# A DiT block's query projection: four full products per band pair against seven products of halves, with the projections before attention in another order

## The chip, the cores and the metric

The kernel runs on one core of a Trainium2 chip. The metric is the device time of one execution in microseconds (us). A core has a TensorE (PE; its weight loads are listed as PEld), a VectorE (DVE), a ScalarE (ACT), a GpSimd (POOL) and a SyncE (SP). All five have in-order instruction queues. SP's queue does nothing but start DMAs here; ACT and POOL start some too.

## The reference

One layer of a diffusion transformer on 1024 latent tokens and 256 context tokens, width 1024, all in float32:

```
h_x = rmsnorm(x)*(1+sc1)+sh1;   h_c = the same of ctx          # sh, sc, gt: a vector times w_mod
u, q, k, v = split(h_x @ w_in)  (512 columns each); k_c, v_c = the same of h_c
attn = neighbourhood_attention(q, k, v, k_c, v_c, rpb)          # 8 heads of 64, clamped 8 x 16 window + context keys
mix  = concat(pool_mixer(u), attn) @ w_out                      # pools of 2, 4, 8, 16 tokens minus the token
x    = x + gt1*rmsnorm(mix)
out  = x + gt2*rmsnorm(relu(modulate(x) @ w_mlp_in)**2 @ w_mlp_out)
```

The change touches q = h_x[1024, 1024] @ w_in[:, 512:1024] and the place of u, v and the pool mixer's small products in the order of the work. Queries are needed for the latent tokens only.

## The kernel before, in words

**Precision.** A float32 product is done as three products in a shorter type. Every operand is split into a high half (ACT copies it with rounding, `split` L143) and a low half (DVE subtracts the high half from the source). `three` (L193) issues the three matmuls high·high, high·low and low·high into one PSUM bank (512 columns of float32). A 128-deep step of a 128 x 512 result is thus three matmuls; a result with 1024 terms is 8 steps or 24 matmuls.

**Operands.** The normalised latent tokens, transposed, lie in eight tiles `xT[k]` (k is a block of 128 features). `latent(b, k)` (L411) makes from them, for the token halves b = 0 and 1, the modulated operand `hx[b][k]`, high and low half side by side; `modulated` (L198) writes the float32 value into a passing buffer `tmp1`. The context tokens become `hc[k]`. Weights come by `load` (L172, one 512 KB DMA on SP into one of the raw buffers `wraw`) and `high_low` (L177) into buffers `whl`.

**Order on TensorE before attention.** Keys `pk` (L433), the transposes of the context tokens `pct`, keys of the context `pkc` (96 matmuls of 256 columns), values of the context `pvc` (48), values `pv` (8 banks of 24, L583), pool channels `pu` (8 banks of 24, L651), queries of token half 0 and of the first head pair of half 1 `pq` (L715, 120), the products of the pools `py` (24, `pool_out` L638), one more bank of queries, and then the attention units, the first two of which have a bank of queries behind them (L984). Two head pairs of 64 features are one block j of 128; q is thus 4 blocks j by 2 token halves b, 8 banks of 24 matmuls or 192 in all. ACT copies each out of PSUM with the factor -1/8 (L710).

**Background work.** The other modulation vectors (sh2, sc2, gt1, gt2: names sh, sc, a, b) are made beside this: GpSimd zeroes `acc` and loads a bias row into it (`mod_sum` L211, L212), VectorE adds eight blocks of `w_mod` (L216, 128 x 1024 each, one 512 KB load each), and four small matmuls `pgsh`, `pgsc`, `pga`, `pgb` (L223) add up over the partitions. `background(n)` (L511) says how many of these steps stand behind a bank of products.

**Pools.** `pooled(g)` (L602) is VectorE work on `u`. Its two halves are split into `d` and multiplied by `pool_w` (`py`); ACT scales the result (L645) into `y`, and for token half 0 it and VectorE also make the operand `mix` of the output projection straight from PSUM (L648, L649).

**Attention.** 32 units, (block j, band m of 128 tokens). `scores` (L737, products L753) write a bank pair; VectorE adds a table and takes the minimum (L767); ACT takes the exponential (L776); PE transposes (L795) and multiplies by the values (L829). The tables (`tables(j)`, L684) are made by GpSimd, 12 subtractions (L695), from the mask (`mask_page`, L675) and a load of `rpb` into `U`. In this stage the order of PE, ACT, DVE and SP is fixed by `in_order` (L104), and PSUM holds two score bank pairs and four other banks.

**The output projection and the MLP** already use a seven-product form with sums of quarters (names A11, A12, A22, S1 to S4 for the left operand, B11, B21, B22, T1 to T4 for the right). Accumulating DMAs on GpSimd (`add_to`, L910) make such sums in SBUF.

Of the kernel before, what the change touches and what calls it, by code (L numbers as in the profile page):

```python
# [80 lines left out]
def hybrid_block(ctx, tc, x, ctx_in, w_mod, b_mod, gp1, gp2, w_in, pool_w, rpb, w_out, w1, w2, vectors,  # L81
# [61 lines left out]
    def split(src, hi, lo):  # L143
        nc.scalar.copy(hi, src)
        nc.vector.tensor_tensor(lo, src, hi.bitcast(F32), sub)
# [9 lines left out]
    def step_split(src, hi, lo, less=False):  # L155
        if less:
            nc.scalar.activation(hi, src, AF.Copy, scale=-1.0)
        else:
            nc.scalar.copy(hi, src)  # L159

        def second():
            if less:
                nc.vector.scalar_tensor_tensor(lo, src, -1.0, hi.bitcast(F32), mul, sub)
            else:
                nc.vector.tensor_tensor(lo, src, hi.bitcast(F32), sub)  # L165

        if stepwise:
            behind.append(second)
        else:
            second()  # L170
# [6 lines left out]
    def high_low(name, raw):  # L177
        hi = whl.tile([P, 1024], F32R, tag="hl", name=f"{name}h")
        lo = whl.tile([P, 1024], F32R, tag="hl", name=f"{name}l")
        split(raw, hi, lo)  # L180
        return hi, lo

    def weights(name, src):
        return high_low(name, load(name, src))
# [13 lines left out]
    def modulated(tmp, name, src, scale, shift, hi, lo, n, on_act=False):  # L198
        h = tmp.tile([P, 512], F32, tag="t", name=f"{name}t")
        if on_act:  # L200
            nc.scalar.activation(h[:, :n], src, AF.Identity, bias=shift, scale=scale)
            nc.scalar.copy(hi, h[:, :n])
        else:
            nc.scalar.activation(hi, src, AF.Identity, bias=shift, scale=scale)
            nc.vector.tensor_scalar(h[:, :n], src, scale, shift, mul, add)
        nc.vector.tensor_tensor(lo, h[:, :n], hi.bitcast(F32), sub)
# [20 lines left out]
    def mod_gate(name, acc, gp, bank):  # L227
        g = wraw.tile([P, 1024], F32, tag="raw", name=f"gp{name}w")[:, :256]
# [27 lines left out]
    with tc.tile_pool(name="ps1", bufs=6, space=PSUM) as ps1, tc.tile_pool(name="tmp1", bufs=3) as tmp:  # L256
# [39 lines left out]
        nc.vector.tensor_scalar_add(b_sc, b_sc, 1.0)  # L296
        sT = once("sT", [P, KT, 32])
# [100 lines left out]
        def shift_scale(q, mr):  # L398
            pt = bank(f"pmt{q}")
            for j in range(2):  # L400
                nc.tensor.matmul(pt[:, 4 * j : 4 * j + 4], mr[:, j * P : (j + 1) * P], pck, start=True, stop=True)
            pv = pt[:, :8].rearrange("p (j w v) -> p w v j", w=2, v=2)
            hs = slice(2 * q, 2 * q + 2)
            for v in range(2):
                nc.vector.tensor_tensor(a1[v][:, hs], pv[:, 1, v], b_sc[:, hs], add)
                nc.vector.tensor_tensor(a1[v][:, hs], a1[v][:, hs], g1c[:, hs], mul)
                nc.vector.tensor_tensor(s1[v][:, hs], pv[:, 0, v], b_sh[:, hs], add)
# [3 lines left out]
        def latent(b, k):  # L411
            src = xT[k][:, b * 512 : (b + 1) * 512]
            h = page(f"hx{b}_{k}", F32R)
            modulated(tmp, f"hx{b}_{k}", src, a1[0][:, k : k + 1], s1[0][:, k : k + 1], h[:, :512], h[:, 512:], 512,
                      on_act=(b == 1))
            hx[b][k] = h
# [49 lines left out]
        for q in range(4):  # L466
# [3 lines left out]
            if q < 3:  # L470
                mr = mod_rows(q + 1)
                wgt.append(high_low(f"wk{q + 1}", raw_k[q + 1]))
# [5 lines left out]
            if q < 3:  # L478
                latents(q + 1)
        for j in range(4):  # L480
            kept_keys(0, j)
        for i, t in enumerate(cp):
            squares(f"c{i}", t)
        for i, t in enumerate(cp):
            normalised(f"c{i}", t)
# [36 lines left out]
        def mod_row(name, c, gp):  # L522
# [3 lines left out]
            def close():  # L526
                mod_gate(name, acc, gp, bank)
# [23 lines left out]
        def in_group(name, c0):  # L551
            return [weights(f"{name}{kk}", pair(w_in, kk, c0, 512)) for kk in range(KT // 2)]
# [11 lines left out]
        raw_v = [load(f"wv{kk}", pair(w_in, kk, 1536, 512)) for kk in range(KT // 2)]  # L564
        for j in range(4):
# [3 lines left out]
            if j == 3:  # L569
                wgt = [high_low(f"wv{kk}", raw_v[kk]) for kk in range(KT // 2)]  # L570
            nc.scalar.copy(kc[:, j], ps)
        startup.close()
        with tc.issue_after(last[ET.DVE]):
            background(4)
        vcp = page("vc")
        for i in range(2):
            ps = bank(f"pvc{i}")
            token_group(ps, wgt, ctx_tok(i))
            nc.scalar.copy(vcp[:, i * 512 : (i + 1) * 512], ps)
            background()  # L580

        vp = [page(f"v{i}") for i in range(4)]
        for m in range(NM):  # L583
            ps = bank(f"pv{m}")
            token_group(ps, wgt, lat_tok(m // 4, m % 4))
            if m == 5:
                raw_u = [load(f"wu{kk}", pair(w_in, kk, 0, 512)) for kk in range(KT // 2)]
            if m == NM - 1:
                wgt = [high_low(f"wu{kk}", raw_u[kk]) for kk in range(KT // 2)]
            nc.scalar.copy(vp[m // 2][:, (m % 2) * 512 : (m % 2) * 512 + 512], ps)  # L590
            if m < 5:
                background(4)
        vb = [vp[m // 2][:, (m % 2) * 512 : (m % 2) * 512 + 512] for m in range(NM)]

# [41 lines left out]
        nc.vector.tensor_scalar_mul(npcol, pscol, -1.0)  # L636

        def pool_out(g):  # L638
            y = pools[g] = page(f"y{g}")
            for b in range(2):  # L640
# [5 lines left out]
                if b == 0:  # L646
                    mp = mix["A11"][g] = wraw.tile([P, 1024], F32R, tag="raw", name=f"mix0_{g}")
                    nc.scalar.activation(mp[:, :512], ps, AF.Identity, scale=pscol[:, g : g + 1])  # L648
                    nc.vector.scalar_tensor_tensor(mp[:, 512:], ps, pscol[:, g : g + 1], mp[:, :512].bitcast(F32), mul, sub)  # L649

        for g in range(4):  # L651
            up = page(f"u{g}")
            for b in range(2):
# [8 lines left out]
                background(2)  # L662
            dv = pooled(g, up).rearrange("p (r m c) -> p m r c", r=QR, m=NM)
            dT.append([])
            for b in range(2):
# [3 lines left out]
                split(dv[:, 4 * b : 4 * b + 4], bands(hi), bands(lo))  # L669
                dT[g].append((hi, lo))  # L670

# [3 lines left out]
        def mask_page():  # L675
# [3 lines left out]
            for i in range(2):  # L679
                tabs.append([page(f"tab{i}{e}") for e in range(2)])  # L680
                for t in tabs[i]:
                    nc.gpsimd.memset(t[:, NLOC:NKEY], 0.0)

        def tables(j):  # L684
            u = page(f"U{j}").rearrange("p (e t) -> p e t", e=2)
# [14 lines left out]
        wgt = in_group("wq", 512)  # L700
        qT = [[None] * 2 for _ in range(4)]
        qp = {}

        def queries(j, b, ps, n):
            feature_group(ps, wgt, j * P, b, range(KT))
            if j % 2 == 0:
                qp[b] = page(f"q{b}_{j}")
            qT[j][b] = qp[b][:, (j % 2) * 512 : (j % 2) * 512 + 512]
            background(n)
            nc.scalar.activation(qT[j][b].rearrange("p (m t) -> p m t", t=P)[:, :, ::-1],  # L710
                                 ps.rearrange("p (m t) -> p m t", t=P), AF.Identity, scale=-(HD ** -0.5))

        pools = [None] * 4
        mix = {n: [None] * 4 for n in ("A11", "A12", "A22", "S1", "S2", "S3", "S4")}
        for j in range(4):  # L715
            queries(j, 0, bank(f"pq{j}_0"), (1, 2, 3, 99)[j])
        mask_page()
        tables(0)
        with in_order(ET.PE) as pooling:
            queries(0, 1, bank("pq0_1"), 0)  # L720
            for g in range(4):
                pool_out(g)


    with (
# [184 lines left out]
        def add_to(to, more):  # L910
            nc.gpsimd.dma_start(to, more, accum_op=add)

# [9 lines left out]
        first_pool.__enter__()  # L922
        with in_order(ET.PE, ET.Activation, ET.DVE, ET.SP) as projected:
            with tc.issue_after(pooling[ET.PE]):
                queries(1, 1, bank("pq1_1"), 0)
            for i in range(N + 4):
# [18 lines left out]
                if i in (1, 2):  # L945
                    for k in (2 * i - 2, 2 * i - 1):
                        add_to(s3[k], s1a[k])
# [35 lines left out]
                if i < 2:  # L983
                    queries(2 + i, 1, bank(f"pq{2 + i}_1"), 0)  # L984
# [31 lines left out]
    with tc.tile_pool(name="ps2", bufs=6, space=PSUM) as ps2:  # L1016
# [6 lines left out]
      with ExitStack() as tmp2:  # L1023
# [117 lines left out]
        nc.vector.scalar_tensor_tensor(a2, scale2, 1.0, g2c, add, mul)  # L1141
        less_a2, less_s2 = sm("na2", 8), sm("ns2", 8)
        nc.vector.tensor_scalar_mul(less_a2, a2, -1.0)
        nc.vector.tensor_scalar_mul(less_s2, s2, -1.0)
# [144 lines left out]
        def weight_parts(p, which):  # L1289
# [13 lines left out]
            for n in which:  # L1303
# [10 lines left out]
                step_split(src, blocks(w[:, :512]), blocks(w[:, 512:]), n in ("A12", "A22"))  # L1314
# [400 lines left out]
```

## Time and profile before

| what | number |
|---|---|
| median of 3 runs | 1044.83 us (1044.76 to 1044.93) |
| the profiled execution's own time | 1044.82 us |
| its span in the trace | 1043.0 us (1.8 us lie around it) |
| PE busy | 1029.6 us, 99% of the span |
| DVE, ACT, POOL busy | 711.6, 530.8, 96.4 us |
| mean granted clock of TensorE | 0.997 of full speed |

A row of a timeline reads: start, duration, engine, line, operation, output<-inputs, shape, count, and in brackets the idle time of the engine just before with what ended it. A row of windows gives the busy time of each engine in a stretch of the span, and the share of time in which the DMA engines were busy. A row of DMA issues gives a transfer's size and the time from its issue to its landing. Durations of matmuls overlap: the step from one start to the next is the cost.

### The profile page before, as it was taken

What the parts mean: (1) busy time and instruction counts of PE and PEld (TensorE: products, weight loads), DVE (VectorE), ACT (ScalarE), POOL (GpSimd) and SP (SyncE); (2) the same over time, 40 slices, a digit from 0 to 9 for tenths busy, and PEclk for the clock granted to TensorE, in tenths of its full rate; (3) what the DMA queues carried; (4) which work ended last, traced back from release to release, by engine and by line L of the source; (5) the groups of instructions that cost most, each with busy time, mean ns of one, the idle gap of its engine ahead of it and who ended that gap; (6) DMA issues with size and microseconds to landing.
All of it is one profiled execution on the core that took longest, in us unless ns stands there. A gap on an engine that the chain in (4) does not pass through costs nothing.

```text
span 1043.0 us, 15532 instructions
## 1 busy us (share of the span) xinstructions
PE 1029.6 (99%) x5862; PEld 846.0 (81%) x5862; DVE 711.6 (68%) x1118; ACT 530.8 (51%) x923; POOL 96.4 (9%) x155
## 2 busy tenths in 40 slices
PE   8999999999999999999999999999999999999996
PEld 6788788877888888887888888888888888888885
DVE  5535657536897588878998876764676666547586
ACT  7553121247888465876655555545553334334441
POOL 3010200041331203320000000000000000000001
PEclk9999999999999999999999999999999999999998
DMA  9905764033337696595786553445787766655556
GB/s 341 337 21 178 270 216 135 21 75 100 64 81 189 160 218 203 189 250 167 263 271 231 193 191 129 156 139 192 268 325 264 234 230 222 200 173 194 175 187 201
DMA packets 108155, 199.61 MB, mean 191 GB/s; under 512 B 8496, under 2 KB 45104, under 8 KB 108080
## 3 DMA queue, kind: packets, MB, share of 16 engines
q1 hardware_dynamic: 84544, 152.92, 44.7%
q10 hardware_dynamic: 17136, 30.97, 8.0%
q0 software_dynamic: 6400, 14.72, 6.7%
q8 instruction: 46, 0.75, 0.3%
q14 instruction: 29, 0.24, 0.1%
HBM read 149.81 MB, written 39.34 MB: 181 GB/s over the span
## 4 chain that ended last, share of the span: by engine, by line
PE 96%; ACT 1%; DMA 1%; DVE 1%; issue 0%; SPq 0%; DVEq 0%; POOLq 0%; ACTq 0%
PE pk L433 4%; PE S L753 3%; PE pa L829 3%; PE phv L194 3%; PE phz L194 3%; PE phx L194 3%; PE pyv L196 3%; PE phz L195 3%; PE pyz L196 3%; PE pyx L194 3%; PE phx L195 3%; PE phv L195 3%; PE pyx L196 3%; PE phx L196 3%; PE pyv L194 3%; PE pyz L195 3%
## 5 line engine op out<-in xcount | busy, mean ns | idle before, releaser
L140 POOL TENSOR_TENSOR ry<-vy,nhalf 128x1 f32<-128x1 f32 x8 | 4.4, 551 | 570.8 <-DVE vy L138 570.8
L776 ACT ACTIVATE sp<-sp,nm 128x640 f32<-128x640 f32 (+1 forms) x64 | 51.4, 803 | 9.5 <-DVE nm L767 8.7
L767 DVE CUSTOM_DVE_ANT_0 sp<-S,tab 128x640 f32<-128x640 f32 (+1 forms) x56 | 42.8, 802 | 17.9 <-PE S L753 11.3
L1328 ACT ACTIVATE c<-c 128x512 f32<-128x512 f32 x48 | 30.3, 632 | 46.2 <-DVE c L1448 21.6
L159 ACT CAST wpS<-S 128x512 fp32r<-128x512 f32 x64 | 38.6, 616 | 27.8 <-PE phv L196 9.4
L165 DVE TENSOR_TENSOR wpS<-S,wpS 128x512 fp32r<-128x512 f32 x64 | 43.5, 686 | 10.4 <-ACT wpS L159 10.4
L194 PE MATMUL phx<-thB,wpA 128*128 128x512 f32 x128 | 50.2, 392 | 0.0
L195 PE MATMUL phx<-tlB,wpA 128*128 128x512 f32 x128 | 49.8, 389 | 0.0
L196 PE MATMUL phx<-thB,wpA 128*128 128x512 f32 x128 | 49.8, 389 | 0.0
L1329 ACT ACTIVATE c<-c 128x512 f32<-128x512 f32 x48 | 30.3, 631 | 15.3 <-DVE sa L1411 12.1
L194 PEld LDWEIGHTS phx<-thB,wpA 128*128 128x128 f32 x128 | 24.0, 188 | 5.5 <-ACT s L1379 0.5
L753 PE MATMUL S<-kT,q 64*128 64x384 f32 (+1 forms) x128 | 28.0, 495 | 0.4 <-DVE nm L767 0.4
L196 PEld LDWEIGHTS phx<-thB,wpA 128*128 128x128 f32 x128 | 24.0, 188 | 5.1
L195 PEld LDWEIGHTS phx<-tlB,wpA 128*128 128x128 f32 x128 | 24.0, 188 | 4.8
L829 PE MATMUL pa<-pt,v 128*64 128x128 f32 x352 | 25.9, 279 | 0.7 <-ACT px L809 0.3
L814 DVE COPY pt<-T 128x512 f32<-128x512 f32 x32 | 21.9, 685 | 5.5 <-PE T L795 5.5
L194 PE MATMUL phz<-thB,wpS 128*128 128x512 f32 x64 | 25.0, 391 | 0.0
L194 PE MATMUL phv<-thT,wpA 128*128 128x512 f32 x64 | 25.0, 391 | 0.0
L196 PE MATMUL phv<-thT,wpA 128*128 128x512 f32 x64 | 24.9, 389 | 0.0
L195 PE MATMUL phz<-tlB,wpS 128*128 128x512 f32 x64 | 24.9, 389 | 0.0
L194 PE MATMUL phy<-thT,wpS 128*128 128x512 f32 x64 | 24.9, 389 | 0.0
L195 PE MATMUL phy<-tlT,wpS 128*128 128x512 f32 x64 | 24.9, 389 | 0.0
(1039 smaller groups left out, 3326.3 us busy)
## 6 DMA issues: line engine op xcount, KB each, us to landing
b<-in_w SPq DMA_DIRECT2D x64, 512.0 KB, 4.3
hrS<-hdS SPq DMA_DIRECT2D x32, 512.0 KB, 5.5
hrA<-hdA SPq DMA_DIRECT2D x24, 512.0 KB, 5.6
wm<-in_w_mod SPq DMA_DIRECT2D x16, 512.0 KB, 9.6
wa_0w<-in_w SPq DMA_DIRECT2D x16, 512.0 KB, 5.1
wa_1w<-in_w SPq DMA_DIRECT2D x16, 512.0 KB, 4.2
hdA<-c ACTq DMA_DIRECT2D x32, 256.0 KB, 2.4
hdS<-sa ACTq DMA_DIRECT2D x32, 256.0 KB, 2.6
```

The source lines that it names most:

```text
L159: nc.scalar.copy(hi, src)
L165: nc.vector.tensor_tensor(lo, src, hi.bitcast(F32), sub)
L194: nc.tensor.matmul(ps, ahi, bhi, start=first, stop=False, skip_group_check=more)
L195: nc.tensor.matmul(ps, ahi, blo, start=False, stop=False, skip_group_check=more)
L196: nc.tensor.matmul(ps, alo, bhi, start=False, stop=last, skip_group_check=more)
L433: nc.tensor.matmul(pks[b][j], wk(wgt, k, low, j * P, P), r, start=(k == 0 and n == 0), stop=(k == KT - 1 and n == 2))
L753: nc.tensor.matmul(S[e][:, c0 : c0 + keys.shape[1]], q[hs, cols], keys[hs], start=True, stop=True)
L767: nc.vector.tensor_tensor_reduce(out=to, in0=s, in1=bt, scale=1.0, scalar=BIG, op0=add, op1=ALU.min, accum_out=nm)
L776: nc.scalar.activation(sp, sp, AF.Exp, bias=least[i, e], scale=-1.0, accum_out=sums[i][:, e : e + 1])
L829: nc.tensor.matmul(pa[e * HD : (e + 1) * HD, cols], v[:, f : f + HD], turns[i][:, e, c] if c < 4 else fifths[i][:, :, (e + 1) * HD : (e + ...
L1328: nc.scalar.activation(r, src, AF.Relu)
L1329: nc.scalar.activation(r, r, AF.Square)
```

## The change

**Queries.** q is seen as two row blocks (token halves) by two column blocks (head pairs 0-1 and 2-3), with the sum over features in two halves. Seven products of such quarters replace eight: A11·B11, A12·B21, S2·T2, S1·T1, S4·B22, S3·T3, A22·T4. Each is two banks of 4 steps, 24 matmuls; seven are 168. Copies on ACT and ten additions on VectorE (three kinds, new L823, L832, L841, L1109, L1111) put the results together in place in the query tiles; the bank of A11·B11 stays in PSUM and gets A12·B21 added, that of S1·T1 gets S4·B22.

**Sums of tokens.** The second half of the gain vector `g1c` and the matching weights change sign, so that the four sums of tokens are plain additions. `modulated` writes its float32 value over `xT` (argument `kept`). VectorE then adds 128 x 512 pieces in place: S1 and S3 (eight pieces, with two pieces rebuilt from high and low half) ahead of the normalisation of the context, S2 and S4 (eight pieces) behind it. Each piece goes to DRAM at once (16 stores of 256 KB on SP), comes back later through `tmp1` (which has four buffers, not three), and is split.

**Sums of weights.** Four copies in DRAM on SP (512 KB each) and four accumulating DMAs on GpSimd make T1 to T4 in DRAM: T1 += B11, T3 += B12, T2 += T1, T4 += T2. They stand in GpSimd's queue ahead of the `memset` of `accsh`.

**Order.** TensorE's order is now: keys of the context, `pu`, with `pgsh` in the middle, values of the context, three banks of `pv`, then the four pools' products (`py`, 6 each) between the next banks of `pv`, `pgb`, the products A11·B11, A12·B21, S2·T2, S1·T1, S4·B22, the first scores, S3·T3, the second unit's scores, A22·T4. The operand `mix` of the pools is now split from `y` in SBUF (`pool_mixed`), between the query products. The mask is loaded behind the split of the first piece of S4; the first `U` lies in a raw buffer. From the second unit's query product on, TensorE's order is the one of before, with two additions of queries on VectorE in each of the first two units. The three small operations on `a2` and `s2` (old L1141 and following) are issued behind the attention stage.

```diff
+        def stored_sum(name, place, a, b):
+            stored[name] = dram.tile([P, 4, 512], F32, tag=f"tok{name}", name=f"tok{name}")
+            for i, (to, ai, bi) in enumerate(zip(quarter(place), quarter(a), quarter(b))):
+                nc.vector.tensor_tensor(to, ai, bi, add)
+                nc.sync.dma_start(stored[name][:, i], to)
...
+        with in_order(ET.SP, ET.DVE) as stores:
+            stored_sum("S1", "A22", "A21", "A22")
+            for k in range(2):
+                hi, lo = hx[0][k][:, :512], hx[0][k][:, 512:]
+                nc.vector.tensor_tensor(xT[k][:, :512], hi.bitcast(F32), lo.bitcast(F32), add)
+            stored_sum("S3", "A21", "A21", "A11")
...
+            for n, first in (("T1", "B12"), ("T2", "B22"), ("T3", "B22"), ("T4", "B21")):
+                nc.sync.dma_start(combined[n], query_block(first))
+        for n, more in (("T1", query_block("B11")), ("T3", query_block("B12")), ("T2", combined["T1"]), ("T4", combined["T2"])):
+            add_to(combined[n], more)
...
+        stored_sum("S2", "A11", "A22", "A11")
+        stored_sum("S4", "A12", "A12", "A11")
...
+        with in_order(ET.PE, ET.Pool) as pooling:
+            w11, w21 = (query_weights(n, qraw[n]) for n in ("B11", "B21"))
+            x = [bank(f"pqx{j}") for j in range(2)]
...
+            wb22 = query_weights("B22", qraw["B22"])
+            token_operand("S4", sraw["S4"])
+            mask_page()
+            sraw["S3"] = token_raw("S3")
+            z = [bank(f"pqz{j}") for j in range(2)]
+            queries(1, 2)
+            for j in range(2):
+                query_product(z[j], j, "S1", wt1, True)
+                nc.vector.tensor_tensor(query(2 + j, 1), query(j, 1), by_tile(z[j]), sub)
+            wt3 = query_weights("T3", qraw["T3"])
+            tables(0)
+            token_operand("S3", sraw["S3"])
+            queries(0, 2)
+            for g in range(2):
+                pool_mixed(g)
+            for j in range(2):
+                query_product(z[j], j, "S4", wb22, False)
+                nc.vector.tensor_tensor(query(2 + j, 0), by_tile(z[j]), query(j, 1), sub)
+            wt4 = query_weights("T4", qraw["T4"])
+            for g in range(2, 4):
+                pool_mixed(g)
...
-                queries(2 + i, 1, bank(f"pq{2 + i}_1"), 0)
+                    for j in range(2):
+                        query_product(last_queries[j], j, ("S3", "A22")[i], (wt3, wt4)[i], i == 0)
```

More of the change, by code (lines that the diff above doesn't have):

```diff
@@ L548, in hybrid_block, with in_weights @@
         rest.append(mod_row("b", 5, gp2))
[L551 to L552 removed]
+        def in_weights(name, raw):
+            return [high_low(f"{name}{kk}", r, 1.0 if kk < 2 else -1.0) for kk, r in enumerate(raw)]
         def token_group(ps, w, hk):
@@ L573, in hybrid_block @@
         with tc.issue_after(last[ET.DVE]):
[L574 to L593, printed above, removed]
+            background(6)
         pwt = once("pwt", [P, 4, P])
@@ L636, in hybrid_block @@
         nc.vector.tensor_scalar_mul(npcol, pscol, -1.0)
+        pools = [None] * 4
+        mix = {n: [None] * 4 for n in ("A11", "A12", "A22", "S1", "S2", "S3", "S4")}
         def pool_out(g):
@@ L668, in hybrid_block @@
                 bands = lambda t: t.rearrange("p (m r c) -> p m r c", m=4, r=QR)
-                split(dv[:, 4 * b : 4 * b + 4], bands(hi), bands(lo))
+                split(differences[g][:, 4 * b : 4 * b + 4], bands(hi), bands(lo))
                 dT[g].append((hi, lo))
+        vcp = page("vc")
+        for i in range(2):
+            ps = bank(f"pvc{i}")
+            token_group(ps, wgt, ctx_tok(i))
+            nc.scalar.copy(vcp[:, i * 512 : (i + 1) * 512], ps)
+            background(3)
@@ new lines, in hybrid_block, with token_raw, token_operand @@
+        rows_of = {n: [(hx[b][k][:, :512], hx[b][k][:, 512:]) for k in range(4 * kh, 4 * kh + 4)]
+                   for n, b, kh in (("A11", 0, 0), ("A12", 0, 1), ("A22", 1, 1))}
+        def token_raw(name):
+            raw = [tmp.tile([P, 512], F32, tag="t", name=f"{name}r{i}") for i in range(4)]
+            for i in range(4):
+                nc.sync.dma_start(raw[i], stored[name][:, i])
+            return raw
+        def token_operand(name, raw):
+            rows_of[name] = []
+            for i in range(4):
+                h = page(f"{name}h{i}", F32R)
+                split(raw[i], h[:, :512], h[:, 512:])
+                rows_of[name].append((h[:, :512], h[:, 512:]))
@@ new lines, in query_raw, with query_weights, query_product @@
+        def query_raw(name):
+            return load(f"wq{name}", combined[name] if name in combined else query_block(name))
+        def query_weights(name, raw):
+            return high_low(f"wq{name}", raw, (-1.0 if name == "B11" else 1.0) * HD ** -0.5)
+        def query_product(ps, j, a, w, begin):
+            hi, lo = w
+            for k in range(4):
+                o = k * 256 + j * P
+                three(ps, hi[:, o : o + P], lo[:, o : o + P], *rows_of[a][k], begin and k == 0, k == 3, more=not begin)
@@ new lines, in hybrid_block @@
+        vp = [page(f"v{i}") for i in range(4)]
+        qraw, sraw = {}, {}
+        for n, m in enumerate((4, 5, 6, 7, 0, 1, 2, 3)):
+            ps = bank(f"pv{m}")
+            token_group(ps, wgt, lat_tok(m // 4, m % 4))
+            nc.scalar.copy(vp[m // 2][:, (m % 2) * 512 : (m % 2) * 512 + 512], ps)
+            background(2)
+            if 2 <= n < 6:
+                difference_split(n - 2)
+            if n == 1:
+                sraw["S2"] = token_raw("S2")
+            if 3 <= n < 7:
+                pool_out(n - 3)
+            if n == 6:
+                for w in ("B11", "B21", "T2", "T1"):
+                    qraw[w] = query_raw(w)
+                token_operand("S2", sraw["S2"])
+                sraw["S1"] = token_raw("S1")
@@ L673, in hybrid_block @@
+        background(99)
+        vb = [vp[m // 2][:, (m % 2) * 512 : (m % 2) * 512 + 512] for m in range(NM)]
         tabs, msk = [], []
@@ L713, in hybrid_block, with queries @@
[L713 to L722, printed above, removed]
+        def queries(b, j):
+            qp = page(f"q{b}_{j}")
+            qT[j][b], qT[j + 1][b] = qp[:, :512], qp[:, 512:]
```

171 lines of the change are left out of this document (104 added, 67 removed).

## The prediction

> **What bounds the kernel now.** I read first the busy times on the page, then what TensorE (PE) waited for, then windows over the stage that the change rebuilds.
>
> ```profile
> PE 1029.6 (99%) x5862; PEld 846.0 (81%) x5862; DVE 711.6 (68%) x1118; ACT 530.8 (51%) x923; POOL 96.4 (9%) x155
> ```
>
> ```profile
> PE pxt L324 <- POOL ident masks.py:199: 1.6, 1, 1.6
> ```
>
> ```profile
> 52.00:78.00 26.00, 26.00 (x132) 22.04 (x131) 9.93 (x24) 14.82 (x29) 4.57 (x6) 1.00 0.06 21
> 104.00:130.00 26.00, 26.00 (x125) 20.39 (x124) 16.78 (x14) 3.69 (x7) 5.66 (x10) 1.00 0.78 269
> 208.00:234.00 26.00, 26.00 (x117) 20.82 (x116) 10.56 (x16) 12.87 (x24) 10.82 (x26) 1.00 0.31 75
> ```
>
> PE is busy 99% of the span, and its longest wait in the whole trace, at the start, is 1.6 us. In the windows the first busy column is PE's: 26.00 of 26 in each, at full clock (1.00). So a matmul taken out of this stage is worth its whole duration, and any new wait of PE costs its whole length. VectorE (DVE), the third column, has 9 to 16 us free per window, ScalarE (ACT) 11 to 22. The DMA engines (the last but one column) are nearly idle from 52 to 78, and 0.78 busy from 104 to 130.
>
> **The change part by part.** *Matmuls.* ACT copies each bank of 24 matmuls when it is done, so the distance of two copies is the price of a bank:
>
> ```profile
> 104.84 0.59 ACT L590 COPY v<-pv 128x512 f32<-128x512 f32 x1 [4.85 <-PE pv L196]
> 110.28 0.59 ACT L590 COPY v<-pv 128x512 f32<-128x512 f32 x1 [4.85 <-PE pv L196]
> ```
>
> 5.44 us for 24 is 0.2267 each. Queries go from 192 matmuls to 168; values, pools and the four sums over partitions only change places. **This removes 24 x 0.2267 = 5.44 us.** Ahead of the first scores (S of unit 0) stood 144 query matmuls (120, and the bank behind `py`), now 120; two banks of 24 follow in both. So unit 0 moves forward by the whole gain:
>
> ```profile
> 88.10 0.39 PE L194 MATMUL pvc<-wv0h,hc 128*128 128x512 f32 x1
> ...
> 227.86 0.70 PE L753 MATMUL S<-kcT,q 64*128 64x256 f32 x4
> ```
>
> If nothing waits, it starts at 227.86 - 5.44 = 222.4, and the query products, 120 x 0.2267 = 27.2 us, start at 195.2. The sum of pieces between 88.1 and there is otherwise the old one.
>
> *Token sums ahead of the context (58 to 73).*
>
> ```profile
> 57.75 0.69 DVE L206 TENSOR_TENSOR hx<-hx_7t,hx 128x512 fp32r<-128x512 f32 x1 [0.68 <-ACT hx L202]
> 63.77 0.15 DVE L136 TENSOR_SCALAR vt_c<-ms_c 128x1 f32<-128x1 f32 x1 [5.32 <-ACT jkc L131]
> ...
> 72.31 0.43 DVE L206 TENSOR_TENSOR hc<-hc0t,hc 128x256 fp32r<-128x256 f32 x1 [4.82 <-ACT hc L202]
> ```
>
> Ten additions at 0.69 fill 58.4 to 65.3 where DVE stood idle for 5.32 us; the context's normalisation slips by up to 1.5 us. Eight more fit the idle 4.82 us up to 72.31 but for some 2 us, and the chain of `hc` behind it has idle time before each DVE step. I cost this at 0; if the cover is short, up to 1.5 us appears before the keys of the context. Writing `hx` in place only shares a tile with its own reader: 0.
>
> *Weight sums in DRAM.* GpSimd (POOL) starts T1, T3, T2, T4 and only then zeroes `accsh` and fetches its bias. T2 waits for T1's landing, T4 for T2's. DVE's first `accsh` sum waits for the bias, all DVE work behind it too, and PE's `pgsh` for the eighth sum.
>
> ```profile
> 66.00 0.95 POOL L211 MEMSET accsh<- 128x1024 f32 x1
> ...
> 69.23 0.52 POOL L212 DMA_DIRECT2D accsc<-in_b_mod  x1 [0.31 <-DMA accsh<-in_b_mod]
> ```
>
> ```profile
> 99.60 1.28 DVE L216 SCALAR_TENSOR_TENSOR accsh<-wmsh_4w,sx,accsh 128x1024 f32<-128x1024 f32 x1 [0.53 <-DMA wmsh_4w<-in_w_mod]
> 100.92 1.29 DVE L216 SCALAR_TENSOR_TENSOR accsh<-wmsh_5w,sx,accsh 128x1024 f32<-128x1024 f32 x1
> ```
>
> ```profile
> sb<-hdA SPq DMA_DIRECT2D x10, 256.0 KB, 5.2
> ...
> ss<-y SPq DMA_DIRECT2D x4, 256.0 KB, 3.1
> ...
> nf<-nf POOLq DMA_DIRECT2D x2, 512.0 KB, 6.4
> ...
> to_0w<-in_w_out SPq DMA_DIRECT2D x1, 512.0 KB, 4.2
> ...
> to_0w<-in_w_out POOLq DMA_DIRECT2D x1, 512.0 KB, 11.2
> to_1w<-in_w_out POOLq DMA_DIRECT2D x1, 512.0 KB, 13.2
> to_2w<-to_0w POOLq DMA_DIRECT2D x1, 512.0 KB, 9.0
> ...
> to_3w<-in_w_out POOLq DMA_DIRECT2D x1, 512.0 KB, 12.1
> msk<-in_mask SPq DMA_DIRECT2D x1, 384.0 KB, 2.9
> ```
>
> The copy for T1 is issued at about 65.5, behind eight stores of 256 KB; with 4.2 (its row of a load of that size) to some 7 us for it, T1 starts near 71. Let X be the landing times of T1 and T2 together. From memset to bias landed is 66.00 to 69.23 = 3.2 us, and an issue ahead of it 0.9: the sums can start at 71 + X + 4.1. Eight at the distance of 1.32 take 10.6. PE's `pgsh` stands behind four banks: 88.1 + 4 x 5.44 = 109.9. So no stall while X is under 24. The nearest rows (the same kind of sum, 512 KB, landing in SBUF) give 2 x 6.4 = 12.8, 11.2 + 9.0 = 20.2 and 13.2 + 12.1 = 25.3. A sum that lands in DRAM is in no row. I take X under 24 and cost 0, nearest to the pair T1, T2 in kind (20.2); the ends are 0 and 1.1, or more if DRAM is slower (rival B).
>
> [...]
>
> *The later background sums* are paced by the banks and slip forward and back with them; `accsc` must be done by `pgsc` behind the context's values, at 88.1 + 10 x 5.44 = 142.5. Sixteen sums at 1.32 are 21 us of the 50 till then, which leaves DVE 29 for the first pools' additions: 0.
>
> *Query stage, 195.2 to 222.4.* Work per 27.2 us: ACT has 12 token and 4 pool splits, 4 weight casts and 5 copies; DVE 16 low halves, 4 weight low halves, 6 additions.
>
> ```profile
> L144 ACT CAST S<-y 128x512 fp32r<-128x512 f32 x8 | 5.0, 625 | 1.5 <-DVE S L145 1.5
> L144 ACT CAST t_0h<-b 128x1024 fp32r<-128x1024 f32 x3 | 3.2, 1055 | 10.3 <-PE pyy L195 3.4 <-PE pyx L195 3.4 <-PE pyv L195 3.4
> L163 DVE SCALAR_TENSOR_TENSOR wpA<-wa_1w,wpA 128x512 fp32r<-128x512 f32 x22 | 15.1, 688 | 2.7 <-ACT wpA L157 2.7
> ```
>
> ```profile
> 221.65 2.51 POOL L695 TENSOR_TENSOR tab<-msk,U 128x128 f32<-128x128 f32 x6 [6.22 <-DMA U<-in_rpb]
> 224.10 0.88 POOL L911 DMA_DIRECT2D y<-y  x1
> 224.76 2.73 POOL L695 TENSOR_TENSOR tab<-msk,U 128x128 f32<-128x128 f32 x6
> ```
>
> ```profile
> 223.72 0.75 DVE L649 SCALAR_TENSOR_TENSOR mix<-py,cols,mix 128x512 fp32r<-128x512 f32 x1 [0.99 <-ACT mix L648]
> ```
>
> ACT: 16 x 0.625 + 4 x 1.055 + 5 x 0.59 = 17.2 us. DVE: 16 x 0.69 + 4 x 1.28 (the row of `accsh`, also two inputs of 128 x 1024) + 6 x 0.75 (PSUM in, as the row of `mix`) = 20.7 us. Both fit 27.2, DVE with 24% to spare.
>
> *The new wait.* S of unit 0 goes into the bank pair that holds z1, the second bank of S4·B22. It must wait until DVE has taken z1 out (new L841): the last product ends at 222.4, the addition takes 0.75 and two hand-overs 0.15, so **0.9 us at least**. That addition stands on DVE behind the low half of the last pool operand, `mix_3`, whose raw buffer held `U` until the first tables are done. The chain: the second bank of A12·B21 ends at 195.2 + 10.9 = 206.1; ACT copies it (0.6) and casts S4's first piece (0.63); DVE takes its low half (0.69): 208.1, or 209.4 if the piece, requested near 205 at 3.1 us, lands at 208. On SP the mask stands behind the third sums' first load, which waits for that split; it is issued at 209.8 and lands 2.9 later, 212.7. Twelve table steps, 2.51 + 2.73 = 5.2: 217.9. ACT splits `mix_3` and one piece of S3: 219.2; DVE two low halves and the addition for z0: 221.3. That is 1.1 us early, so the floor of 0.9 stands. With 5.2 for the piece of S4 and 4.2 for the mask (the row of 512 KB) the chain is 3.4 later and the wait 0.9 + 2.3 = 3.2. Queues on DVE and ACT between these steps, not free in my count, lie between. I take **1.5 us**, nearer to the lower end.
>
> *Behind it* DVE has two additions of 0.75 per bank of 5.44 us in units 0 and 1: hidden. The second tables and the pool sums start as much later or earlier as unit 0 does. The moved `a2` steps have no one waiting: 0.
>
> **Sum**: 1044.82 (the profiled execution; the median of the runs is 0.01 above it) - 5.44 + 1.5 = 1040.9 us.
>
> **The rivals.** *A, the tables are slowed (other end of the wait).* DVE is busy 76% of the query stage, mostly with two SBUF inputs, while GpSimd makes the tables; in the trace of before they ran beside little DVE work (10.56 us in 26), the six steps beside the `mix` row at 2.73 against 2.51. Doubled, the chain is 5.2 later, which is 4.1 behind the floor: a wait of 5.0 in place of 1.5, 1044.4; slowed by half, 2.4, 1041.8. It costs from 21% on, where the 1.1 is used up. For it: no row shows the tables beside such work. Against: the rise seen is 9%. [...]
>
> *B, slower: the DRAM sums.* If accumulating in DRAM takes 18 us each (half again 12.1), X is 36 and PE waits 12 us at `pgsh`: 1052.9. It decides from X = 24; the gain is eaten at 28, and from 30 the kernel is slower by more than 0.2%. For it: the chain of landings, stores and copies at the same time. Against: DMA share 0.06 there.
>
> *C, background sums or an operand late by 1 to 3 us at `pgsc`, `pga` or a query product:* 1042 to 1044. For it: six new meeting points with 1 to 4 us to spare by my count.
>
> *D, the shorter product does nothing else:* all waits hidden, 1044.8 - 5.4 = 1039.4; it needs scores that don't wait for z1's bank. That the gain is fully eaten (no change) is A or C at its upper end.
>
> **How the numbers follow.** Forecast (1039.9 to 1042.6) 0.60; A 0.12; B 0.11; C 0.13; D 0.04. A measurement here tells about 0.2% (2.1 us) from no change: 1042.7 to 1046.9 is "same". Faster: 0.60 + 0.04 + half of A + half of C = 0.77, taken as 0.72 since some meeting point may have been missed; same: the rest of A and C and the mild end of B, 0.15; slower: most of B, and what was missed, 0.13. The range 1039.3 to 1046.0 leaves out B and little of the rest.
>
> **What would show it.** Right: PE has one wait of 0.9 to 3 us at S of unit 0, released by DVE's L841; S of unit 0 starts near 223.9; the query stage is 27.2 us long without idle PE. The sum is wrong if PE idles at `pgsh` (B: POOL's memset of `accsh` after 96), if the tables take over 7 us (A), or if PE waits elsewhere between 88 and 222 (C). A wait of PE before 88 would show the cover of the token sums too short.

## The result, and the profile after

The changed kernel takes 1050.4 us (median of 10 runs, 1046.93 to 1051.95), the kernel before 1044.83 us beside it (1044.64 to 1045.61). The ratio is 1.0047, 95% interval 1.0034 to 1.006: slower, where 1040.9 was predicted (1039.3 to 1046.0). The profiled execution took 1051.88 us, 7.06 more than that of before; the accounts below are made against it.

TensorE (PE) does less work: its instructions fell by 24 and its busy time from 1029.6 to 1029.3 us, although, as will be seen, part of that time is at half clock. What is new stands in PE's waits (waited for, total, times, longest):

```profile
PE pgsh L227 <- DVE accsh L220: 4.3, 1, 4.3
PE S L875 <- DVE q L841: 2.4, 1, 2.4
...
PE pqz L198 <- DVE q L832: 0.9, 1, 0.9
```

And in the windows of before (busy times of PE, PEld, DVE, ACT, POOL, then granted clock, DMA share, GB/s; the second fence is the one window of the kernel before that was not shown yet):

```profile
52.00:78.00 26.00, 26.00 (x132) 22.01 (x131) 20.06 (x42) 14.75 (x29) 4.09 (x4) 1.00 0.77 241
78.00:104.00 26.00, 26.00 (x156) 23.26 (x155) 7.85 (x9) 8.96 (x16) 4.62 (x6) 1.00 0.89 232
104.00:130.00 26.00, 21.69 (x89) 16.77 (x89) 21.81 (x34) 3.25 (x6) 2.85 (x5) 0.87 0.81 262
208.00:234.00 26.00, 22.68 (x99) 18.16 (x99) 18.56 (x25) 13.17 (x22) 10.63 (x18) 0.98 0.52 141
```

```profile
78.00:104.00 26.00, 26.00 (x155) 23.04 (x155) 14.22 (x13) 8.89 (x16) 0.00 (x0) 1.00 0.52 174
```

Up to 104 PE is full, as before. But the DMA share from 52 to 78, 0.06 before, is 0.77; from 78 to 104 it rose from 0.52 to 0.89, and VectorE's busy time there has fallen from 14.22 to 7.85 us: it is waiting for something. From 104 to 130 PE loses 4.3 us and, what the prediction had not thought of at all, the granted clock falls to 0.87. A finer table of the same stretch shows how:

```profile
112.00:114.00 2.00, 0.00 (x0) 0.00 (x0) 2.00 (x3) 0.00 (x0) 0.00 (x0) 0.87 0.98 324
114.00:116.00 2.00, 1.57 (x9) 0.70 (x10) 1.97 (x7) 0.38 (x1) 0.00 (x0) 0.50 0.85 258
116.00:118.00 2.00, 2.00 (x6) 1.58 (x5) 1.97 (x3) 0.00 (x0) 1.76 (x4) 0.50 0.90 261
118.00:120.00 2.00, 2.00 (x6) 1.52 (x6) 2.00 (x3) 0.00 (x0) 0.15 (x1) 0.50 0.64 206
120.00:122.00 2.00, 2.00 (x10) 1.60 (x9) 2.00 (x4) 0.00 (x0) 0.00 (x0) 0.92 0.90 310
```

PE idles from 110 to 114.4; the clock goes to 0.50 at 113.5 and comes back at 120.3. PE is "busy" all through 116 to 120, but a window of 2 us has 6 matmuls in it in place of 10: one starts every 0.43 us, not every 0.23. The copies of ACT give the price of the whole event (first the kernel after, then, in the second fence, the kernel before):

```profile
110.16 0.59 ACT L681 COPY u<-pu 128x512 f32<-128x512 f32 x1 [4.33 <-PE pu L200]
115.58 0.38 ACT L579 COPY accsh<-pgsh 128x256 f32<-128x256 f32 x1 [4.83 <-PE pgsh L227]
123.49 0.59 ACT L681 COPY u<-pu 128x512 f32<-128x512 f32 x1 [7.54 <-PE pu L200]
```

```profile
116.52 0.59 ACT L590 COPY v<-pv 128x512 f32<-128x512 f32 x1 [5.27 <-PE pv L196]
```

A bank with `pgsh` ahead of it took 116.52 - 110.28 = 6.24 us before and takes 123.49 - 110.16 = 13.33 now: 7.1 us lost to a wait of 4.3. The same reading at the first scores (S of unit 0): the wait ahead of S4·B22 costs 1.05, that ahead of S 2.5, and from the start of the first scores to those of unit 1 it is 8.3 us (233.01 to 241.32) where it was 6.7, since the clock is at half again from 233 to 236. Together -5.44 + 7.1 + 1.05 + 2.5 + 1.6 = +6.8 of the +7.06.

**Why `pgsh` waited.** GpSimd's (POOL's) timeline, and from the DMA issues the time to landing (us, last column):

```profile
71.58 1.46 POOL L188 DMA_DIRECT2D wqT<-in_w_in  x1 [5.47 <-DMA wqT<-in_w_in]
74.20 1.25 POOL L188 DMA_DIRECT2D wqT<-in_w_in  x1 [1.16 <-DMA wqT<-in_w_in]
84.48 0.84 POOL L188 DMA_DIRECT2D wqT<-wqT  x1 [9.02 <-DMA tokS<-xT]
91.68 0.81 POOL L188 DMA_DIRECT2D wqT<-wqT  x1 [6.36 <-DMA wqT<-wqT]
92.21 1.24 POOL L215 MEMSET accsh<- 128x1024 f32 x1
93.75 0.53 POOL L216 DMA_DIRECT2D accsh<-in_b_mod  x1 [0.30 <-DMA wmsh_1w<-in_w_mod]
```

```profile
accsh<-in_b_mod POOLq DMA_DIRECT2D x1, 4.0 KB, 7.6
```

```profile
101.41 1.28 DVE L220 SCALAR_TENSOR_TENSOR accsh<-wmsh_0w,sx,accsh 128x1024 f32<-128x1024 f32 x1 [9.60 <-DMA accsh<-in_b_mod]
...
109.64 1.22 DVE L632 TENSOR_TENSOR sa<-u 128x1023 f32<-128x1023 f32 x1
110.77 1.28 DVE L220 SCALAR_TENSOR_TENSOR accsh<-wmsh_6w,sx,accsh 128x1024 f32<-128x1024 f32 x1
111.97 1.21 DVE L645 SCALAR_TENSOR_TENSOR sb<-sa,u 128x1023 f32<-128x1023 f32 x1
113.10 1.27 DVE L220 SCALAR_TENSOR_TENSOR accsh<-wmsh_7w,sx,accsh 128x1024 f32<-128x1024 f32 x1
```

T1 starts at 71.58 and is landed when T2 starts (84.48); T2 is landed when T4 starts (91.68). (The row at 84.48 names a store of the token sums; T1's own row has 12.6 us from issue to landing, so T1 landed with it.) Only then does `accsh` get its memset. Its bias, a row of 4 KB, takes 7.6 us to land; VectorE sat idle for 9.60 us before the first sum. The token stores had all landed by 84.6. What the bias met was four loads of `w_mod`, issued from 88.4 to 91.8, and T4, issued just ahead of it on the same queue: from 91.7 to 95.4 the trace has packets of the loads' queue alone (they fill 94.7% of the 16 engines' time), then T4's come in, none of the bias before 98.1, and the bias lands at 101.3, 0.2 us behind T4 (91.68 + 9.5 = 101.2). Between the eight sums stand operations of the first pool (L632, L645), so the last ends at 114.4.

**Why the first scores waited.**

```profile
221.57 7.69 POOL L790 TENSOR_TENSOR tab<-msk,U0w 128x128 f32<-128x128 f32 x12 [3.31 <-DMA S3r<-tokS]
```

The row names a load of S3; the mask landed at 221.5 as well (217.2 + 4.3).

```profile
229.29 0.63 ACT L148 ACTIVATE mix<-y 128x512 fp32r<-128x512 f32 x1 [4.45 <-POOL tab L790]
```

```profile
231.07 0.69 DVE L154 SCALAR_TENSOR_TENSOR mix<-y,mix 128x512 fp32r<-128x512 f32 x1
231.68 1.28 DVE L841 TENSOR_TENSOR q<-pqz,q 128x512 f32<-128x512 f32 x2
```

The twelve steps of the first tables take 7.69 us, 5.24 before. ACT's split of `mix_3` waits for them 4.45 us, VectorE's half follows, and only behind it come the two additions that free the bank of the first scores.

### The profile page after: what moved, and what is told of

Same layout as the page of the kernel before. It is cut to its first block, busy times and chain, and to the rows that moved or that the text cites. A ratio compares the mean times of both kernels' runs of the same rounds, so it can differ in the third digit from the quotient of the medians.

```text
span 1050.1 us, 15655 instructions
## 1 busy us (share of the span) xinstructions
PE 1029.3 (98%) x5838; PEld 844.3 (80%) x5838; DVE 741.2 (71%) x1166; ACT 539.7 (51%) x938; POOL 103.3 (10%) x159
## 4 chain that ended last, share of the span: by engine, by line
PE 90%; DMA 4%; DVE 2%; ACT 2%; issue 1%; POOL 1%; SPq 0%; DVEq 0%; POOLq 0%; ACTq 0%
PE pk L441 4%; PE S L875 3%; PE pa L951 3%; PE phv L198 3%; PE phx L198 3%; PE phz L198 3%; PE phv L199 3%; PE pyv L200 3%; PE phz L199 3%; PE pyv L198 3%; PE pyz L200 3%; PE pyz L198 3%; PE pyx L198 3%; PE phx L200 3%; PE phx L199 3%; PE pyx L199 3%
## 5 line engine op out<-in xcount | busy, mean ns | idle before, releaser
L198 PE MATMUL phz<-thB,wpS 128*128 128x512 f32 x64 | 25.0, 391 | 0.0
L199 PE MATMUL phv<-tlT,wpA 128*128 128x512 f32 x64 | 24.9, 390 | 0.0
L200 PE MATMUL phz<-thB,wpS 128*128 128x512 f32 x64 | 24.9, 389 | 0.0
```

The source lines that it names most:

```text
L198: nc.tensor.matmul(ps, ahi, bhi, start=first, stop=False, skip_group_check=more)
L199: nc.tensor.matmul(ps, ahi, blo, start=False, stop=False, skip_group_check=more)
L200: nc.tensor.matmul(ps, alo, bhi, start=False, stop=last, skip_group_check=more)
```

## The experiments

**Each wait taken away, then both.** The theory: two separate losses, one from the place of T2 and T4 in GpSimd's queue, one from `mix_3` ahead of the additions, eat the gain of the products. The rival for each stands in the expectation.

```diff
 # sums_later: T1, T3 stay; T2 and T4 are issued behind accsh's memset and bias
-        with tc.issue_after(last[ET.DVE]):
+        with tc.issue_after(last[ET.DVE]), in_order(ET.Pool) as first_sum:
             background(6)
+        with tc.issue_after(first_sum[ET.Pool]):
+            for n, more in (("T2", combined["T1"]), ("T4", combined["T2"])):
+                add_to(combined[n], more)
 # mix3_later
-            for g in range(2, 4):
-                pool_mixed(g)
+            pool_mixed(2)
...
+                if i == 0:
+                    pool_mixed(3)
                 if i < 2:
```

> The changed kernel with one move: the accumulating DMAs T2 and T4 stand behind the first background sum's memset and bias row in GpSimd's queue, not ahead of them. Theory: the queue held the bias back (memset at 92.2, bias landed at 101.4), and PE's wait of 4.3 us at pgsh with the slow clock behind it (11 products at 0.43 in place of 0.23 us) cost 7.0 us. Then that wait goes and the profiled time falls from 1051.9 to about 1045. Rival: the DMA engines are full with stores and copies (DMA share 0.77 to 0.89 from 52 to 104), so that the bias or the blocks of w_mod land late anyway; then 3 us or more of the wait stay and the time is 1048 or more.

Measured: 1044.36 us (1042.49 to 1045.51, 10 runs; 1043.43 in the profile), ratio to the kernel before 0.9993 (0.9984 to 1.0002). The wait at `pgsh` is gone, and the clock is 1.00 from 104 to 130. The longest wait is now the other one:

```profile
PE S L878 <- DVE q L844: 2.4, 1, 2.4
```

Theory 1045, rival 1048: the theory holds. The rival was right in its premise all the same: the bias, issued at 78.7 now, took 10.8 us to land. It was merely early enough. It landed 0.2 us behind T3, the sum of 512 KB ahead of it on its queue (74.67 + 14.7 = 89.3, and 89.5).

> The changed kernel with one move: the split of the last pool operand, mix_3, is issued in the first attention unit, so that VectorE no longer has it ahead of the addition that frees the bank of the first scores. Theory: the chain over mask, tables and mix_3 made the wait of 2.4 us there; it falls to the 0.9 of the addition alone, the clock dips less or not, and the time falls by 1.5 to 3.5 us from 1051.9, to 1048.4 to 1050.4. Rival: the tables themselves are late (they end at 229.3), VectorE waits for them at the first scores, and PE at the next bank: no gain, 1051 to 1052.

Measured: 1047.89 us (1045.68 to 1049.41, 6 runs), ratio 1.0027 (1.0016 to 1.0039). The profiled execution (1049.41) is within the theory's range, the median 0.5 us below it. Both waits are as the theory has them:

```profile
PE pgsh L227 <- DVE accsh L220: 4.3, 1, 4.3
...
PE S L874 <- DVE q L841: 0.8, 1, 0.8
```

> Both moves together. Theory: two separate losses (7.0 at pgsh, some 5 around the first scores) against a gain of 5.4; with the first gone and the second down to 1 to 2.5: 1041 to 1042.5, faster than before. Rival: the seven products don't give their 5.4 us on the chip (other waits take their place): 1045 or more even with both waits gone.

Measured: 1041.74 us (1040.27 to 1042.09, 8 runs), ratio 0.997 (0.9959 to 0.998). The two losses add up: against the changed kernel's 1050.4 the moves gain 6.0 and 2.5 us alone and 8.7 together. What is left is the gain of the products less 2.4 us. In the profile 1.0 of that are waits of 0.8 at the first scores and 0.2 at S4·B22; another 1.2 stand ahead of all that was moved, where PE waits 1.6 us for `hx` before the keys in place of 0.4 (so too in mix3_later), and no run says why. The rival (the products give nothing on the chip) falls.

**What a wait at `pgsh` costs by itself.** The kernel before, with nothing of the change, and its first background sum held back by 36 memsets in place of one, or by 30 or 33:

```diff
-        nc.gpsimd.memset(acc, 0.0)
+        for _ in range(36 if name == "sh" else 1):
+            nc.gpsimd.memset(acc, 0.0)
```

> The kernel before with 36 memsets of the first background sum's tile in place of one, so that its bias comes some 33 us later and PE waits at pgsh, by about 4 us (0 to 6). It prices such a wait by itself, with no other edit. Theory: the slow clock behind a wait of over 3 us costs some 2.5 us on top: 1044.8 + 4 + 2.5 = 1051. Rival: the wait costs its own length alone (1049), and the slow products in the changed kernel have another cause.

> The kernel before with 30 memsets in place of one (36 gave PE a wait of 8.3 us at pgsh and 10.6 us in the time). At 0.93 us each the wait should be 2.7 us. [...] Rival: the wait costs its own length plus a fixed 2.5 us however short it is: 1050.

> The same with 33 memsets: a wait of about 5.5 us, a little over that of the changed kernel (4.3). Theory: 5.5 plus about 2.5 of slow clock: 1053. Rival (the clock falls only behind longer waits): 1050.3.

The waits came out at 8.3 (36 memsets; about 4 had been meant), 2.2 (30) and 4.9 us (33), the times at 1055.42 (1054.87 to 1056.46, 4 runs, ratio 1.0104, 1.0087 to 1.0121), 1047.52 and 1052.48 us (one run each, beside 1045.11). The copies of ACT around the wait, of 30 and then of 33 memsets:

```profile
110.78 0.58 ACT L591 COPY v<-pv 128x512 f32<-128x512 f32 x1 [4.85 <-PE pv L196]
113.64 0.37 ACT L539 COPY accsh<-pgsh 128x256 f32<-128x256 f32 x1 [2.27 <-PE pgsh L224]
119.31 0.59 ACT L591 COPY v<-pv 128x512 f32<-128x512 f32 x1 [5.30 <-PE pv L196]
```

```profile
110.70 0.59 ACT L591 COPY v<-pv 128x512 f32<-128x512 f32 x1 [4.85 <-PE pv L196]
116.76 0.37 ACT L539 COPY accsh<-pgsh 128x256 f32<-128x256 f32 x1 [5.47 <-PE pgsh L224]
124.35 0.59 ACT L591 COPY v<-pv 128x512 f32<-128x512 f32 x1 [7.22 <-PE pv L196]
```

Against 6.24 without a wait: 8.53, so a wait of 2.2 costs 2.3 and the bank behind it runs at its usual pace (113.64 to 119.31); 13.65, so a wait of 4.9 costs 7.4; with 36 memsets 17.21, so 8.3 costs 11.0. The granted clock is 0.50 behind the two long waits and stays at 1.00 behind the short one. What the slow clock adds is 2.5 us at 4.9 and 2.6 at 8.3, so between these two waits it did not grow. The rival of a fixed cost falls by the short wait; the one that the wait costs only itself falls by the two long ones.

**The changed kernel twice more.**

> The changed kernel once more, for the spread of its runs (1046.9 to 1052.0, most either near 1047 or at 1050 to 1052; the kernel before stays within 1 us). Theory: the time of pgsh's wait hangs on the DMA landings, and what a wait of 2 to 4 us costs hangs on whether the clock falls behind it; in a run near 1047 one of the two stretches at half clock (behind pgsh, behind the first scores) is missing or shorter. Rival: the two waits are the same and the time differs elsewhere (the start, the MLP).

> As the run before, a second look at the same kernel: the same expectations.

Measured: 1049.51 and 1048.6 us (one run each). The wait at `pgsh` is 3.6 us in both, with a stretch of half clock behind it (0.50 from 116 to 118 in the first, from 114 to 116 in the second; 5.3 and 5.1 us lost, by ACT's copies). At the first scores the first execution has a wait of 2.4 and half clock from 231 on; the second has a longer wait, 2.9, and the clock stays at 1.00:

```profile
PE pgsh L227 <- DVE accsh L220: 3.6, 1, 3.6
PE S L875 <- DVE q L841: 2.9, 1, 2.9
```

In sums_later the clock stayed at 1.00 behind a wait of 2.4 too. So part of the spread of this kernel is whether the clock falls behind the second wait, which the wait's length does not decide at 2 to 3 us. Neither time fell near 1047, so which part is missing in those runs stays open.

**Why the bias and T1 were slow.**

```diff
             for i, (to, ai, bi) in enumerate(zip(quarter(place), quarter(a), quarter(b))):
                 nc.vector.tensor_tensor(to, ai, bi, add)
-                nc.sync.dma_start(stored[name][:, i], to)
...
-        with tc.issue_after(stores[ET.SP]):
+        with tc.issue_after(stores[ET.DVE]):
             for n, first in (("T1", "B12"), ("T2", "B22"), ("T3", "B22"), ("T4", "B21")):
...
-                nc.sync.dma_start(raw[i], stored[name][:, i])
+                nc.sync.dma_start(raw[i], w_in[i * P : (i + 1) * P, :512])
```

> The changed kernel without its 16 stores of the token sums to DRAM; the loads that should bring the sums back read rows of w_in instead, so the queries are other numbers. It asks why the bias of the first background sum came so late. Theory (traffic): the stores, the copies and the sums of weights share the DMA engines, so T1 takes 12.9 us from issue to landing and the bias row of 4 KB takes 7.6. Without the stores T1 lands in 6 to 9 us, the bias in 2 to 3, and PE's wait at pgsh of 4.3 us goes: about 1045. Rival (accumulating in DRAM is slow by itself): T1 still takes 11 us or more; then the bias alone is quicker, and some wait may stay.

Measured: 1045.26 us (one run); no wait at `pgsh`; the wait of 2.4 at the first scores stays, with the clock at 0.58 behind it (226 to 228; 0.996 in the mean of the execution, 0.998 in sums_later). Issues of T1, T3, T2, T4 on GpSimd:

```profile
60.34 1.47 POOL L188 DMA_DIRECT2D wqT<-in_w_in  x1 [43.49 <-DMA wqT<-in_w_in]
62.91 1.25 POOL L188 DMA_DIRECT2D wqT<-in_w_in  x1 [1.10 <-DMA wqT<-in_w_in]
67.96 0.84 POOL L188 DMA_DIRECT2D wqT<-wqT  x1 [3.81 <-DMA wqT<-in_w_in]
...
73.94 0.86 POOL L188 DMA_DIRECT2D wqT<-wqT  x1 [3.71 <-DMA wqT<-wqT]
```

T1 takes 67.96 - 60.34 = 7.6 us where it took 12.9, T2 6.0 where it took 7.2, and everything starts 11 us sooner, because the copies no longer stand behind eight stores on SP. The bias takes 4.7 us, not 2 to 3. The traffic theory holds for T1. The wait it does not settle: of the 17.7 us by which T4 is issued sooner (73.94 against 91.68) 11.2 come from the earlier start and only 6.5 from quicker sums, and either would have covered 4.3; the bias, too, went out before the loads of `w_mod`. Accumulating in DRAM by itself is no slower here (T1 and T3 7.4, T2 and T4 5.6 us to landing, medians of two) than the rows of before that land in SBUF (6.4 to 13.2).

**The tables beside VectorE (rival A by itself).** In the kernel before, eight extra VectorE operations of 128 x 512, two behind each `mix`, where GpSimd makes the first tables; the control has `nc.vector.tensor_scalar_mul(more, ps, 2.0)` in place of the addition:

```diff
+                    for _ in range(2):
+                        more = tmp.tile([P, 512], F32, tag="t", name=f"more{g}")
+                        nc.vector.tensor_tensor(more, mp[:, :512].bitcast(F32), mp[:, 512:].bitcast(F32), add)
```

> The kernel before with eight more VectorE additions of 128 x 512, both inputs in SBUF, results unused, two behind each mix operand, where GpSimd makes the first tables. It prices rival A by itself: in the changed kernel the 12 steps took 7.7 us beside such VectorE work, before 5.2. Theory: the two engines get in each other's way at SBUF; the 12 steps take 6 to 8 us here. Rival: the steps were slow from something else (the mask or the raw buffer of U); they take 5.2 to 5.5.

> The same place and number of additional VectorE operations of 128 x 512, but with one input, in PSUM: the control. Theory: only inputs in SBUF matter; the 12 steps take 5.2 to 5.5 us as in the kernel before. Rival: any VectorE work beside slows them; 6 us or more.

The two halves of the tables, with both inputs in SBUF, then with the input in PSUM:

```profile
222.03 3.90 POOL L698 TENSOR_TENSOR tab<-msk,U 128x128 f32<-128x128 f32 x6 [6.11 <-DMA U<-in_rpb]
...
226.54 4.15 POOL L698 TENSOR_TENSOR tab<-msk,U 128x128 f32<-128x128 f32 x6
```

```profile
221.91 2.50 POOL L698 TENSOR_TENSOR tab<-msk,U 128x128 f32<-128x128 f32 x6 [6.00 <-DMA U<-in_rpb]
...
225.02 2.73 POOL L698 TENSOR_TENSOR tab<-msk,U 128x128 f32<-128x128 f32 x6
```

8.05 us against 5.23, with 5.24 in the kernel before. Both theories hold: these subtractions of GpSimd were slowed beside VectorE's additions with two inputs in SBUF and not beside as many operations that read PSUM (an operation with one input in SBUF was not tried). Why the one slows the other no run shows. The times of these two, 1045.48 and 1045.84 (one run each), tell nothing; their tables are off the critical path.

**A version that beats both.** Both moves, the banks of S1·T1 and S4·B22 in the two lasting banks, so that the first scores don't meet them, and the split of `mix_2` moved as well (shown against both_later):

```diff
-            if name[:2] == "pm" or name in ("pxt1_0", ...
+            if name[:2] == "pm" or name[:3] == "pqz" or name in ("pxt1_0", ...
...
-            pool_mixed(2)
...
-                    pool_mixed(3)
+                    for g in (2, 3):
+                        pool_mixed(g)
```

> Both moves of the run before, and two more: the banks of S1·T1 and S4·B22 come from the two lasting banks, so that the first scores need not wait for VectorE, and the split of the third pool operand also goes into the first attention unit. Theory: the last 0.8 us at the first scores and the 0.2 at S4·B22 go, 1 us in all: 1040 to 1041.3, ratio 0.995 to 0.997. Rival: the wait only moves, to the first product of S3·T3, which now uses the same banks: 1041.5 to 1042.5.

Measured: 1040.5 us (1039.92 to 1040.89, 5 runs), ratio 0.9956 (0.9942 to 0.9969). PE's busy time is 1023.9 us, 5.7 below before, and behind the keys no wait is longer than 0.3 us; S of unit 0 starts at 222.69, 5.2 before the old time. What is left:

```profile
PE pa L952 <- ACT px L932: 0.4, 2, 0.2
PE S L876 <- DVE nm L890: 0.3, 1, 0.3
```

The theory holds, and the rival's wait at S3·T3 did not come. The time is 4.6 us below the kernel before beside it (1045.14), so most of the 5.44 of the seven products can be had; the order and the places in the queues decide it.

## Why the prediction was wrong, step by step

- **Matmuls, -5.44 us: right.** With the waits gone (own_banks) the first scores start 5.2 us earlier, and the time is 4.6 lower.
- **Token sums ahead of the context at 0: right.** No wait stands between 52 and 104.
- **Weight sums in DRAM at 0: wrong, and the step that turned the sign.** It was written that T1 starts near 71 and that X, T1 and T2 together, is 20.2: it was 71.6 and 12.9 + 7.2 = 20.1. What failed is the step behind it, "From memset to bias landed is 66.00 to 69.23 = 3.2 us": it was 92.21 to 101.41 = 9.2. That row came from a stretch in which the DMA engines were nearly idle (share 0.06). By the prediction's own sum the bias goes out near 92, where the share was 0.52 already before and is 0.89 now; and it counted T4 ahead of the bias with the 0.9 us of its issue, not with its landing, 0.2 us behind which the bias came. How much of the 6.0 is T4 and how much the other traffic no run separates. The second failing term is "Eight at the distance of 1.32 take 10.6": 101.41 to 114.37 = 13.0, since two operations of the first pool of 1.2 us each stand between the sums. (The kernel before took 13.0 for its eight as well, 92.33 to 105.37, there for the blocks of `w_mod`; the 1.32 was its closest pair.) 6.0 + 2.4 more, less the 4.1 us that X left to spare, is the 4.3 of the wait. Rival B had the place and the victim right, the cause (sums in DRAM of 18 us each, memset after 96) wrong: X was 20.1, the memset at 92.2, and without the stores the four sums land in 5.6 (T2, T4) and 7.4 us (T1, T3). That the time came out near B's 1052.9 is luck.
- **The price of a wait.** That "any new wait of PE costs its whole length" holds for 2.2 us (2.3) and fails for 4.3 (7.1), with the clock at 0.50 from 113.5 to 120.3.
- **The new wait at the first scores, 1.5: the place and chain were right, the size not.** Tables 7.69 for 5.24, the mask 4.3 for 2.9 to land; the wait was 2.4, plus 0.9 ahead of S4·B22 and 1.6 of half clock. That tables are slowed beside such VectorE work is shown by the pair of table runs (8.05 against 5.23); that rival A's price for tables slowed by half was 2.4 as well is partly luck, since that rival had neither the late mask nor the 1.05 us that PE lost just before. The floor of 0.9 was right: 0.8 once `mix_3` was out of the way.
- **Query stage, work fits 27.2 us: nearly.** One meeting point of rival C came true, S4·B22 behind L832, with 0.9 us.
- **Range and chances.** The range ended at 1046 because the slower case was tied to X from 24 on; no other way to a late bias was counted, and no price above a wait's own length.

The granted clock was 0.50 behind five of the six waits of 3.6 to 8.3 us; behind the sixth (mix3_later, 4.3) it was 0.87 in the mean of 104 to 130, as in the changed kernel. Of the four profiles with a wait of 2.4 three had a slow clock behind it (0.50 in the changed kernel and in its first repetition, 0.58 over 226 to 228 in no_stores) and one had 1.00 (sums_later), as had the one with 2.9: at these lengths the length does not decide, and what does was not shown. Behind `pgsh` in the changed kernel the half clock cost 2.8 us: 10 matmuls at 0.43 in place of 0.23 make 2.0, `pgsh` and the first matmul behind it 0.7.

## What to carry to other kernels

A DMA's time to landing belonged here to the traffic around it, what stood ahead of it on its own queue included, and not to its size alone (1.9 to 10.8 us for the same 4 KB): when a change adds transfers, the small ones that someone waits for must be priced again at the new load, and issued ahead of the large ones in their queue (the bias ahead of T2 and T4 alone: 1044.36 us for 1050.4). Count an in-order queue (GpSimd's here, with the memset at 92.21 right behind T4 at 91.68) from the change's last instruction to the first old one behind it, and then everything between the operations that are waited for. On this kernel, whose TensorE is 99% busy, waits of 3.6 to 8.3 us cost 1.5 to 2.8 us beyond their length in five profiles, and that of 2.4 in the changed kernel 1.6, so two small misses turned a gain of 5 us into a loss of 5 to 6.

## What the runs showed of the hardware that I had not expected

- A bias row of 4 KB took 1.9 us to land with the DMA engines nearly idle (share 0.06), 4.7 without the token stores, 7.6 in the changed kernel and 10.8 when it was issued while the stores were landing; in the last two it landed 0.2 us behind the accumulating DMA of 512 KB issued ahead of it on its queue.
- In the changed kernel the granted clock went to 0.50 while TensorE waited (at 113.5), and stayed there for 5.9 us after it resumed (114.4 to 120.3); the loss was 2.5 and 2.6 us for waits of 4.9 and 8.3, none (0.1) for 2.2, and 1.5 to 2.8 for 3.6 to 4.3. Behind a wait of 2.4 it fell in three profiles of four (to 0.50 in two, 0.58 over 2 us in the third), and cost 1.6 in the changed kernel.
- Twelve GpSimd subtractions of 128 x 128 took 5.23 us beside VectorE operations that read PSUM and 8.05 beside VectorE operations with two inputs in SBUF; in the changed kernel, beside VectorE work mostly of the second kind, 7.69.
